# y of a gMLP encoder transposed by 32x32 blocks on all partitions at once, with transfers joining the quarters

## The chip, the core and the metric

The kernel runs on one core of one Trainium2 chip. The metric is the device time in microseconds of one execution; a kernel's time is the median of several. Profiles come from one further execution each. Engines are named as in the profile: PE (matrix multiply), PEld (its weight loads), DVE (vector engine), ACT (activations), POOL (which here issues transfers and little else), SP (which only issues transfers).

## What is computed

One layer of a gMLP encoder in float32: 1024 tokens, model width D = 2048, inner width E = 4096, eight groups of 512 channels, chunks of 128 tokens.

```python
h = rmsnorm(x, a_norm)
u, v, gate = split(h @ w_in, 3)          # w_in: (2048, 3 * 4096)
u = gelu(u)
v = rmsnorm(gelu(v), v_gain)
sv = einsum('gpq,bnqgc->bnpgc', w_s, v_chunks) + b_s    # per chunk n of 128 tokens, per group g
y = u * sv
x = x + (y * silu(gate)) @ w_out         # w_out: (4096, 2048)
out = rmsnorm(x, final_norm)
```

The output projection contracts over the 4096 channels. The matrix unit contracts over partitions, so y, which is made with tokens on partitions, is needed with channels on partitions.

## The kernel before, in words

Both large products are done as a Strassen product of 2x2 blocks: seven products `p` instead of eight, of sums and differences of blocks (`A_OF` and `B_OF` name the blocks; 11, 12, 21, 22). Every float32 operand is split into a high part that the matrix unit takes in its fast format (`hi`, made by ACT, L88) and a rest (`lo`, made by DVE, L89), and `mm3` (L93 to L95) multiplies hi x hi, hi x lo and lo x hi into the same bank. A **step** is one block of 256 rows of the contraction (two halves `u` of 128) for four chunks `m` of 128 tokens: 2 x 4 x 3 = 24 matmuls of 128x512.

The work runs in this order. Four strips make v; eight gate strips, one for each group g, make u and the gate of 512 channels each; each strip has 7 products of 4 steps. Then the output stage runs the seven products of `OUT_ORDER` for two column pairs s, 8 steps each. `advance(i)` prefetches the raw operands three steps ahead (`prefetch`) and splits those of two steps ahead (`feed`); SP issues the loads of weights, POOL those of y (`load_y`) and v. Instructions of an engine run in the order in which they were placed, so DVE's `w_lo` of a step stands behind whatever was placed before it.

In a gate strip the gate product of a half (512 tokens, four chunks m) is finished in the sixth or seventh product; then `apply_spatial` multiplies by w_s on PE and DVE forms y in place, one 128x512 instruction for each m (L325). After that y is transposed. A DVE transposition works on blocks of 32x32 within 32 partitions. `finish_y` does one 32-token part of one chunk with four instructions on 32 partitions each (L354), which put every block at its place in a full transpose: `yt` has channels on its 128 partitions and tokens in order along the row. When two chunks are done, one transfer of 512 KB on POOL's queue writes `yt` to `y_dram[g][half]` (L358), 128 partitions with runs of 256 tokens (1 KB).

The transpositions are not placed at once but put on the list `later` with a planned cost (L329: 16 items of 1.2 for a half, four instructions each). After each step `work(us)` takes items until the budget is used up: 2.3 in a gate strip and in the output stage for s = 1; for s = 0 it is 1.1 when the product's A operand is one block and 0.6 when it is a sum. In the output stage additions to the result (L492) are put ahead of them in the list. `load_y` (L143) asks, for the last group, whether all 32 writes of y have been issued, and if not places everything that is on the list.

Buffers of 4 KB a partition come in pools: "big" (25) for raw operands and output tiles, "ax" (16) for activations, operands of y and the transposed tiles, "hl" (6) for split weights, "sum" (3).

In the output stage `feed` splits y with the same `split` as the weights; `products` takes `ah[:, u, t]`, 128 consecutive tokens of chunk m, as the stationary operand.

Of the kernel before, what the change touches and what calls it, by code (L numbers as in the profile page):

```python
# [7 lines left out]
F32 = mybir.dt.float32  # L8
F32R = mybir.dt.float32r
AF = mybir.ActivationFunctionType  # L10
ALU = mybir.AluOpType
# [21 lines left out]
def gmlp_kernel(ctx, tc, x, xT, g_in, w_in, gain, wsT, bsT, w_out, fnorm, out):  # L33
# [9 lines left out]
    JI = D // P // 4  # L43
    JO = E // P // 4
    NV = G // 2
    AHEAD, LOADS = 2, 3

    main = ctx.enter_context(tc.tile_pool(name="main", bufs=1))
# [37 lines left out]
    def split(raw, hi, lo):  # L86

        nc.scalar.activation(out=hi, in_=raw, func=AF.Copy)  # L88
        nc.vector.tensor_tensor(out=lo, in0=raw, in1=hi.bitcast(F32), op=ALU.subtract)  # L89

    def mm3(acc, ah, al, bh, bl, start, stop, on=False):

        nc.tensor.matmul(out=acc, lhsT=ah, rhs=bh, start=start, stop=False, skip_group_check=on)  # L93
        nc.tensor.matmul(out=acc, lhsT=ah, rhs=bl, start=False, stop=False, skip_group_check=on)  # L94
        nc.tensor.matmul(out=acc, lhsT=al, rhs=bh, start=False, stop=stop, skip_group_check=on)  # L95
# [16 lines left out]
    steps += [("out", s, p, j) for p in OUT_ORDER for s in range(len(outs)) for j in range(JO)]  # L112

    v_dram = [[dram.tile([P, HCH, C], F32, tag=f"v{g}_{h}", name=f"v{g}_{h}") for h in range(2)] for g in range(G)]
    y_dram = [[dram.tile([P, CB, HT], F32, tag=f"y{g}_{h}", name=f"y{g}_{h}") for h in range(2)] for g in range(G)]
    a_dram = {(p, j): [dram.tile([P, 2, HT], F32, tag=f"a{p}_{j}{l}", name=f"a{p}_{j}{l}") for l in "hl"]
              for p in IN_ORDER for j in range(JI)}

# [3 lines left out]
    def load_w(step, block):  # L122
        kind, s, p, j = step
        mat, cols, n = (w_in, strips, JI) if kind == "in" else (w_out, outs, JO)
        cached = kind == "in" and (s > 0 or block == 22)
        key = (kind, s, 0 if cached else p, block, j)
        if key not in wraw:
            k = ((block // 10 - 1) * n + j) * 2 * P
            col = cols[s][block % 10 - 1]
            wraw[key] = slot("big", "w_raw")  # L130
            nc.sync.dma_start(
                out=wraw[key], in_=mat[k:k + 2 * P, col:col + C].rearrange("(u p) c -> p u c", p=P))
        return wraw[key]

    def load_y(step, block):
        _, _, p, j = step
        key = (p, block, j)
        if key not in yraw:
            g, b = divmod(((block % 10 - 1) * JO + j) * 2, CB)
            if g == G - 1 and pairs_of_y[0] < 4 * G:  # L140
                work_all()
            yraw[key] = slot("big", "y_raw")
            nc.gpsimd.dma_start(out=yraw[key], in_=y_dram[g][block // 10 - 1][:, b:b + 2, :])  # L143
        return yraw[key]

    def prefetch(i):
# [44 lines left out]
    def feed(i):  # L191

        if i >= len(steps):
            return
        kind, s, p, j = step = steps[i]
        first = kind == "in" and s == 0
        if first or (kind == "out" and s == 0):
            load = h_block if first else load_y
            raw = combine(A_OF[p], lambda b: load(step, b), "sum", "a_sum")


            out_j = j if kind == "out" else -1
            tag = "big" if (p == OUT_ORDER[0] and out_j >= JO - 4) or (p == OUT_ORDER[-1] and out_j == JO - 1) else "ax"
            parts = [slot(tag, f"a_{l}", F32R) for l in ("hi", "lo")]
            split(raw, *parts)
            aparts[i] = parts
            if first:
                for t, d in zip(parts, a_dram[p, j]):
                    nc.gpsimd.dma_start(out=d, in_=t.bitcast(F32))
        elif kind == "out":  # L210
            aparts[i] = aparts[i - JO]
        raw = combine(B_OF[p], lambda b: load_w(step, b), "sum", "w_sum")
        wparts[i] = [slot("hl", f"w_{l}", F32R) for l in ("hi", "lo")]
        split(raw, *wparts[i])
# [72 lines left out]
        inv_rms(ssv_t, E, rv)  # L287


    Q = 32  # L290
    spatial = {}

    def load_v(g, c):
# [22 lines left out]
    def apply_spatial(g, half, n_set, prod):  # L316
        banks = bank_set(n_set, f"sv{g}_{half}")
        for m in range(HCH):
            sv = banks[m // 2][:, m % 2]
            wh, wl, vh, vl = spatial[half * HCH + m]  # L320
            mm3(sv, wh, wl, vh, vl, True, True)
        for m in range(HCH):
            sv = banks[m // 2][:, m % 2]
            y = prod[m // 2][:, m % 2]
            nc.vector.scalar_tensor_tensor(  # L325
                out=y, in0=sv, scalar=bs_sb[:, g:g + 1], in1=y, op0=ALU.add, op1=ALU.mult)
        for m in range(HCH):
            for part in range(P // Q):
                later.append((1.2, lambda m=m, part=part: finish_y(g, half, m, part, prod[m // 2])))  # L329

    def spatial_step(k, g, cs, n_set):

# [10 lines left out]

    yts = {}

    def finish_y(g, half, m, i, y):

        t, c = divmod(m, 2)
        if c == 0 and i == 0:
            yts[0] = slot("ax", "y_t").rearrange("p a (b c) -> p (a b) c", c=2 * P)  # L350
        yt = yts[0]
        yv = y[:, c].rearrange("t (b q c) -> t b q c", b=CB, q=P // Q)
        for q in range(P // Q):
            nc.vector.transpose(  # L354
                out=yt[q * Q:(q + 1) * Q, :, c * P + i * Q:c * P + (i + 1) * Q],
                in_=yv[i * Q:(i + 1) * Q, :, q, :])
        if c == 1 and i == P // Q - 1:
            nc.gpsimd.dma_start(out=y_dram[g][half][:, :, 2 * t * P:2 * (t + 1) * P], in_=yt)  # L358
            pairs_of_y[0] += 1

    pairs_of_y = [0]


    def products(i, banks, fresh, ms=range(4)):
        _, _, p, j = steps[i]
        (ah, al), (bh, bl) = aparts[i], wparts[i]
        last = j == (JI if i < n_in else JO) - 1
        for u in range(2):
            for m in ms:
                t = slice(m * P, (m + 1) * P)  # L370
                mm3(banks[m // 2][:, m % 2], ah[:, u, t], al[:, u, t], bh[:, u], bl[:, u],
                    fresh and j == 0 and u == 0, last and u == 1, not fresh)

    def advance(i):
# [97 lines left out]


    NB = D // C
    sso = [main.tile([P, HCH, NB], F32, tag=f"sso{h}", name=f"sso{h}") for h in range(2)]
    acc = {}
    fn_b = []
# [2 lines left out]
    def init_acc(s, block):  # L480
        if (s, block) in acc:
            return
        acc[s, block] = [slot("big", f"o{block}_{t}") for t in range(2)]
        col = outs[s][block % 10 - 1]
        for t in range(2):
            r0 = ((block // 10 - 1) * HCH + 2 * t) * P
            nc.gpsimd.dma_start(
                out=acc[s, block][t], in_=x[r0:r0 + 2 * P, col:col + C].rearrange("(u p) c -> p u c", p=P))

    def add_to(s, block, sign, t, banks):  # L490
        d = acc[s, block][t]
# [26 lines left out]
    def finish_rows(h, m):  # L518

        ro = ros.pop((h, m))  # L520
        r0 = (h * HCH + m) * P
        for s in range(2):
            for n in range(2):
                block = 10 * (h + 1) + n + 1
# [5 lines left out]
                else:  # L530
                    nc.scalar.activation(out=d, in_=d, func=AF.Copy, scale=ro)
                col = outs[s][n]
                nc.sync.dma_start(out=out[r0:r0 + P, col:col + C], in_=d)

    n_set = a
    for p in OUT_ORDER:
# [91 lines left out]
```

## Time and profile before

| | |
|---|---|
| median of 3 runs | 2563.28 us (2563.18 to 2563.37) |
| profiled execution | 2561.8 us, its span 2560.0 us |
| mean granted clock of PE | 0.995 of full speed |
| busy: PE, PEld, DVE, ACT, POOL | 98%, 81%, 70%, 33%, 7% |
| moved by DMA | 695.62 MB, mean 272 GB/s |

The span runs from the first to the last instruction in the trace; the time of the execution is a little longer. Busy shares are averages over stages that differ. Matmuls are pipelined: each is recorded for longer than the distance to the next, so whether PE loses time is read from the distance between starts, not from its busy share. A wait is shown in brackets behind the row of the instruction that waited, with the engine and line that ended it.

### The profile page before, as it was taken

How to read it: one execution, taken by the hardware profiler on the slowest of the kernel's cores; microseconds unless marked ns; L12 is line 12 of the kernel's file. 1: busy time of each engine (PE TensorE's matmuls, PEld its weight loads, DVE VectorE, ACT ScalarE, POOL GpSimd, SP SyncE). 2: the span in 40 equal slices, each digit the busy share in tenths (PEclk: the TensorE clock that was granted, in tenths of full speed). 3: DMA queues.
4: the chain of work that ended last, by engine and by line, in shares of the span. 5: the costliest groups of instructions: out<-in, count | busy, mean ns of one | idle time of the engine just before them, and what ended most of it. 6: DMA issues, size and time to landing. Idle time of an engine off the chain costs nothing.

```text
span 2560.0 us, 29690 instructions
## 1 busy us (share of the span) xinstructions
PE 2514.0 (98%) x10980; PEld 2062.0 (81%) x10980; DVE 1797.8 (70%) x2469; ACT 856.3 (33%) x1008; POOL 167.3 (7%) x290
## 2 busy tenths in 40 slices
PE   7999999999999999999999999999999999999998
PEld 4878888888888888888888888888888788888886
DVE  7974544545448869588595886958769855576795
ACT  4542332323324242232423324233243232232342
POOL 1210000000000000000000000000010110010010
PEclk8999999999999999999999999999999999999999
DMA  8897785958767685766858668586696875678885
GB/s 316 315 411 286 274 313 201 381 204 329 281 254 272 230 336 200 288 260 241 328 203 294 253 242 336 194 307 248 223 362 209 298 257 173 223 263 284 298 294 189
DMA packets 246784, 695.62 MB, mean 272 GB/s; under 512 B 21472, under 2 KB 21488, under 8 KB 246640
## 3 DMA queue, kind: packets, MB, share of 16 engines
q1 hardware_dynamic: 207552, 551.62, 59.7%
q0 software_dynamic: 39088, 142.11, 15.0%
q8 instruction: 87, 1.43, 0.2%
q14 instruction: 57, 0.47, 0.1%
HBM read 622.34 MB, written 71.30 MB: 271 GB/s over the span
## 4 chain that ended last, share of the span: by engine, by line
PE 76%; DVE 16%; issue 5%; DMA 2%; ACT 1%; POOL 0%; SPq 0%; POOLq 0%; ACTq 0%; DVEq 0%
PE m L94 19%; PE m L93 18%; PE m L95 18%; DVE y_t L354 8%; PE o L94 7%; PE o L93 7%; PE o L95 7%; DVE w_lo L89 3%; DVE w_sum L103 1%; DMA w_raw<-in_w_in 1%; DVE c L325 1%; DMA y_raw<-y 1%; DVE u L431 0%; DVE c L411 0%; ACT w_hi L88 0%
## 5 line engine op out<-in xcount | busy, mean ns | idle before, releaser
L93 PE MATMUL m<-w_hi,a_hi 128*128 128x512 f32 x2688 | 1048.5, 390 | 9.4 <-DVE u L431 4.8
L94 PE MATMUL m<-w_lo,a_hi 128*128 128x512 f32 x2688 | 1049.4, 390 | 4.5 <-DVE w_lo L89 4.5
L95 PE MATMUL m<-w_hi,a_lo 128*128 128x512 f32 x2688 | 1047.9, 390 | 0.2 <-DVE a_lo L89 0.2
L89 DVE TENSOR_TENSOR w_lo<-w_sum,w_hi 128x1024 fp32r<-128x1024 f32 x320 | 391.1, 1222 | 402.9 <-ACT w_hi L88 402.0
L88 ACT ACTIVATE w_hi<-w_sum 128x1024 fp32r<-128x1024 f32 x320 | 339.0, 1060 | 954.2 <-PE m L94 668.9
L93 PEld LDWEIGHTS m<-w_hi,a_hi 128*128 128x128 f32 x2688 | 505.8, 188 | 117.8 <-issue 6.6
L94 PEld LDWEIGHTS m<-w_lo,a_hi 128*128 128x128 f32 x2688 | 505.8, 188 | 114.8 <-DVE w_lo L89 9.8
L95 PEld LDWEIGHTS m<-w_hi,a_lo 128*128 128x128 f32 x2688 | 505.6, 188 | 105.8 <-DVE a_lo L89 0.9
L103 DVE TENSOR_TENSOR w_sum<-w_raw 128x1024 f32<-128x1024 f32 x320 | 389.7, 1222 | 100.5 <-DMA w_raw<-in_w_in 88.3
L94 PE MATMUL o<-w_lo,a_hi 128*128 128x512 f32 x896 | 349.6, 390 | 6.0 <-DVE w_lo L89 6.0
L93 PE MATMUL o<-w_hi,a_hi 128*128 128x512 f32 x896 | 348.7, 389 | 0.8 <-DVE o L575 0.8
L95 PE MATMUL o<-w_hi,a_lo 128*128 128x512 f32 x896 | 348.7, 389 | 0.0
L354 DVE STREAM_TRANSPOSE y_t<-c 32x128 f32<-32x128 f32 x1024 | 309.9, 303 | 15.1
L88 ACT ACTIVATE w_hi<-w_raw 128x1024 fp32r<-128x1024 f32 x128 | 135.9, 1061 | 451.2 <-PE m L94 348.7
L89 DVE TENSOR_TENSOR w_lo<-w_raw,w_hi 128x1024 fp32r<-128x1024 f32 x128 | 155.6, 1216 | 132.8 <-ACT w_hi L88 131.9
L94 PEld LDWEIGHTS o<-w_lo,a_hi 128*128 128x128 f32 x896 | 168.2, 188 | 44.0 <-DVE w_lo L89 9.3
L93 PEld LDWEIGHTS o<-w_hi,a_hi 128*128 128x128 f32 x896 | 168.2, 188 | 36.4 <-DVE o L575 1.5
L95 PEld LDWEIGHTS o<-w_hi,a_lo 128*128 128x128 f32 x896 | 168.2, 188 | 34.7
L88 ACT ACTIVATE a_hi<-a_sum 128x1024 fp32r<-128x1024 f32 (+1 forms) x61 | 63.7, 1044 | 146.4 <-DVE a_sum L103 137.0
L143 POOL DMA_DIRECT2D y_raw<-y x96 | 50.9, 531 | 467.0 <-DVE w_sum L103 245.6
L89 DVE TENSOR_TENSOR a_lo<-a_sum,a_hi 128x1024 fp32r<-128x1024 f32 (+1 forms) x61 | 73.3, 1202 | 10.1 <-ACT a_hi L88 10.1
L358 POOL DMA_DIRECT2D y<-y_t x32 | 23.1, 721 | 727.5 <-DVE y_t L354 727.5
(91 smaller groups left out, 1108.2 us busy)
## 6 DMA issues: line engine op xcount, KB each, us to landing
w_raw<-in_w_in SPq DMA_DIRECT2D x212, 512.0 KB, 6.7
w_raw<-in_w_out SPq DMA_DIRECT2D x192, 512.0 KB, 6.4
y_raw<-y POOLq DMA_DIRECT2D x96, 512.0 KB, 6.3
a_hi<-a_0h SPq DMA_DIRECT2D x77, 512.0 KB, 4.9
a_lo<-a_0l SPq DMA_DIRECT2D x77, 512.0 KB, 5.5
a_hi<-a_1h SPq DMA_DIRECT2D x77, 512.0 KB, 6.4
a_lo<-a_1l SPq DMA_DIRECT2D x77, 512.0 KB, 5.1
a_hi<-a_2h SPq DMA_DIRECT2D x77, 512.0 KB, 6.0
```

Of the source, the lines that this page charges most:

```text
L88: nc.scalar.activation(out=hi, in_=raw, func=AF.Copy)
L89: nc.vector.tensor_tensor(out=lo, in0=raw, in1=hi.bitcast(F32), op=ALU.subtract)
L93: nc.tensor.matmul(out=acc, lhsT=ah, rhs=bh, start=start, stop=False, skip_group_check=on)
L94: nc.tensor.matmul(out=acc, lhsT=ah, rhs=bl, start=False, stop=False, skip_group_check=on)
L95: nc.tensor.matmul(out=acc, lhsT=al, rhs=bh, start=False, stop=stop, skip_group_check=on)
L103: nc.vector.tensor_tensor(out=s, in0=a, in1=b, op=ALU.add if of[1] > 0 else ALU.subtract)
L143: nc.gpsimd.dma_start(out=yraw[key], in_=y_dram[g][block // 10 - 1][:, b:b + 2, :])
L325: nc.vector.scalar_tensor_tensor(out=y, in0=sv, scalar=bs_sb[:, g:g + 1], in1=y, op0=ALU.add, op1=ALU.mult)
L354: nc.vector.transpose(out=yt[q * Q:(q + 1) * Q, :, c * P + i * Q:c * P + (i + 1) * Q], in_=yv[i * Q:(i + 1) * Q, :, q, :])
L358: nc.gpsimd.dma_start(out=y_dram[g][half][:, :, 2 * t * P:2 * (t + 1) * P], in_=yt)
```

## The change

`finish_y` now takes a whole chunk m (128 tokens on 128 partitions) and transposes it with two DVE instructions of 128 partitions x 256 channels each, one for each half n of the group's channels. Each 32x32 block is transposed within its 32 partitions, so partition 32 q + c holds channel c of a block, and tokens 32 q to 32 q + 31 of the chunk. Two tiles (n = 0, 1) collect the four chunks of a half. At the end eight transfers, one for each n and each quarter q of 32 partitions, write 128 KB each in runs of 128 tokens (512 B) to `y_dram`, where the channels of the quarters come together in one row: a row of channel c holds its 512 tokens in the order (q, m, t), t being the token within 32.

`y_dram[g][half]` becomes a plain array of 512 channels x 512 tokens. A load of y puts rows 2p and 2p+1 of a block of 256 on partition p, and so the rows of w_out are loaded in the same order; weights of the first product are loaded as before. `split_y` splits y and puts tokens in order at the same time: ACT writes `hi` in the order (m, u, q, t) with runs of 32, DVE reads the raw tile in runs of 32. `products` takes its 128 tokens of chunk m from that order. In `later` a half has 4 items with a planned cost of 0.8 instead of 16 of 1.2. The accesses to x and out are written with other views of the same rows.

```diff
+    def split_y(raw, hi, lo):
+        rv_, hv = [t.rearrange("p u (q m t) -> p (u q) m t", m=HCH, t=Q) if t is raw else
+                   t.rearrange("p a b -> p (a b)").rearrange("p (m n t) -> p n m t", m=HCH, t=Q) for t in (raw, hi)]
+        nc.scalar.activation(out=hv, in_=rv_, func=AF.Copy)
+        rm, hm, lm = rv_.rearrange("p n m t -> p m n t"), hv.rearrange("p n m t -> p m n t"), None
+        lm = lo.rearrange("p a b -> p (a b)").rearrange("p (m n t) -> p m n t", m=HCH, t=Q)
+        nc.vector.tensor_tensor(out=lm, in0=rm, in1=hm.bitcast(F32), op=ALU.subtract)
...
-    y_dram = [[dram.tile([P, CB, HT], F32, tag=f"y{g}_{h}", name=f"y{g}_{h}") for h in range(2)] for g in range(G)]
+    y_dram = [[dram.tile([C, HT], F32, tag=f"y{g}_{h}", name=f"y{g}_{h}") for h in range(2)] for g in range(G)]
...
-                out=wraw[key], in_=mat[k:k + 2 * P, col:col + C].rearrange("(u p) c -> p u c", p=P))
+            order = "(u p) c -> p u c" if kind == "in" else "(p u) c -> p u c"
+            nc.sync.dma_start(out=wraw[key], in_=mat[k:k + 2 * P, col:col + C].rearrange(order, p=P))
...
-            if g == G - 1 and pairs_of_y[0] < 4 * G:
+            if g == G - 1 and halves_of_y[0] < 2 * G:
                 work_all()
...
-            nc.gpsimd.dma_start(out=yraw[key], in_=y_dram[g][block // 10 - 1][:, b:b + 2, :])
+            nc.gpsimd.dma_start(
+                out=yraw[key], in_=y_dram[g][block // 10 - 1][b * P:(b + 2) * P].rearrange("(p u) t -> p u t", p=P))
...
-            split(raw, *parts)
+            (split if first else split_y)(raw, *parts)
...
         for m in range(HCH):
-            for part in range(P // Q):
-                later.append((1.2, lambda m=m, part=part: finish_y(g, half, m, part, prod[m // 2])))
+            later.append((0.8, lambda m=m: finish_y(g, half, m, prod[m // 2][:, m % 2])))
...
+    def finish_y(g, half, m, y):
+        if m == 0:
+            yts[0] = [slot("ax", f"y_t{n}").rearrange("p a (b c) -> p (a b) c", c=P) for n in range(2)]
+        yv = y.rearrange("t (n b c) -> t n b c", n=2, c=Q)
+        for n in range(2):
+            nc.vector.transpose(out=yts[0][n][:, :, m * Q:(m + 1) * Q], in_=yv[:, n])
+        if m == HCH - 1:
+            yd = y_dram[g][half].rearrange("(n b c) t -> n c b t", n=2, c=Q)
+            for n in range(2):
+                for q in range(P // Q):
+                    nc.gpsimd.dma_start(out=yd[n, :, :, q * P:(q + 1) * P], in_=yts[0][n][q * Q:(q + 1) * Q])
+            halves_of_y[0] += 1
...
+        at = [t.rearrange("p a (m c) -> p a m c", c=P) if i < n_in else
+              t.rearrange("p a b -> p (a b)").rearrange("p (m a c) -> p a m c", a=2, c=P) for t in (ah, al)]
...
-                mm3(banks[m // 2][:, m % 2], ah[:, u, t], al[:, u, t], bh[:, u], bl[:, u],
+                mm3(banks[m // 2][:, m % 2], at[0][:, u, m], at[1][:, u, m], bh[:, u], bl[:, u],
```

## Rows read from the trace of the kernel before

**Rows 1.** The page, part 1: busy us (share of the span) x instructions.
```profile
PE 2514.0 (98%) x10980; PEld 2062.0 (81%) x10980; DVE 1797.8 (70%) x2469; ACT 856.3 (33%) x1008; POOL 167.3 (7%) x290
```

**Rows 2.** Timeline of PE, 1000 to 1012 us: start, duration, instruction, [wait].
```profile
1000.09 0.39 PE L93 MATMUL m<-w_hi,a_hi 128*128 128x512 f32 x1
...
1004.40 0.39 PE L94 MATMUL m<-w_lo,a_hi 128*128 128x512 f32 x1
...
1011.65 0.39 PE L93 MATMUL m<-w_hi,a_hi 128*128 128x512 f32 x1
```

**Rows 3.** Busy time by stretch: length, PE, PEld, DVE, ACT, POOL, clock, DMA share.
```profile
820.00:2050.00 1230.00, 1219.50 (x5355) 1003.11 (x5354) 964.72 (x1633) 394.62 (x415) 59.96 (x97) 1.00 0.73 266
2050.00:2540.00 490.00, 490.00 (x2163) 405.88 (x2162) 330.17 (x309) 156.67 (x193) 46.09 (x81) 1.00 0.72 249
```

**Rows 4.** PE's waits, whole span: us in total, times, longest.
```profile
PE o L94 <- DVE w_lo L89: 6.0, 6, 2.0
...
PE m L94 <- DVE w_lo L89: 4.5, 7, 0.7
```

**Rows 5.** Timeline of PE, a gate strip's late operand.
```profile
1025.93 0.39 PE L93 MATMUL m<-w_hi,a_hi 128*128 128x512 f32 x1
...
1032.63 0.50 PE L94 MATMUL m<-w_lo,a_hi 128*128 128x512 f32 x1 [0.66 <-DVE w_lo L89]
...
1037.98 0.39 PE L93 MATMUL m<-w_hi,a_hi 128*128 128x512 f32 x1
```

**Rows 6.** Timeline of DVE, the same strip.
```profile
996.65 3.79 DVE L354 STREAM_TRANSPOSE y_t<-c 32x128 f32<-32x128 f32 x12
1000.47 1.22 DVE L89 TENSOR_TENSOR w_lo<-w_raw,w_hi 128x1024 fp32r<-128x1024 f32 x1
...
1026.21 2.84 DVE L354 STREAM_TRANSPOSE y_t<-c 32x128 f32<-32x128 f32 x9
1029.09 1.22 DVE L431 TENSOR_TENSOR u<-u,m 128x1024 f32<-128x1024 f32 x1
...
1031.36 1.22 DVE L89 TENSOR_TENSOR w_lo<-w_raw,w_hi 128x1024 fp32r<-128x1024 f32 x1
```

**Rows 7.** Timeline of PE, the output stage's first products.
```profile
1979.53 0.39 PE L93 MATMUL o<-w_hi,a_hi 128*128 128x512 f32 x1
...
2018.24 0.50 PE L94 MATMUL o<-w_lo,a_hi 128*128 128x512 f32 x1 [2.03 <-DVE w_lo L89]
...
2058.63 0.39 PE L93 MATMUL o<-w_hi,a_hi 128*128 128x512 f32 x1
```

**Rows 8.** Timeline of DVE, the output stage before its longest wait.
```profile
1994.49 3.79 DVE L354 STREAM_TRANSPOSE y_t<-c 32x128 f32<-32x128 f32 x12
...
2014.69 1.23 DVE L103 TENSOR_TENSOR a_sum<-y_raw 128x1024 f32<-128x1024 f32 x1 [4.40 <-DMA y_raw<-y]
...
2016.97 1.22 DVE L89 TENSOR_TENSOR w_lo<-w_sum,w_hi 128x1024 fp32r<-128x1024 f32 x1
```

**Rows 9.** Timeline of POOL, the same place.
```profile
2001.09 1.06 POOL L143 DMA_DIRECT2D y_raw<-y  x2 [1.79 <-DVE w_sum L103]
```

**Rows 10.** Groups of instructions: out<-in, shapes, count | busy us, mean ns | idle before.
```profile
L354 DVE STREAM_TRANSPOSE y_t<-c 32x128 f32<-32x128 f32 x1024 | 309.9, 303 | 15.1
...
L325 DVE SCALAR_TENSOR_TENSOR c<-sv,bs_sb,c 128x512 f32<-128x512 f32 x64 | 43.6, 742 | 0.0
...
L311 DVE SCALAR_TENSOR_TENSOR ws_hl<-ws_sb,rv,ws_hl 128x128 fp32r<-128x128 f32 x64 | 19.4, 344 | 0.0
...
L143 POOL DMA_DIRECT2D y_raw<-y x96 | 50.9, 531 | 467.0 <-DVE w_sum L103 245.6 <-PE m L95 70.6 <-DVE a_sum L103 61.7
...
L358 POOL DMA_DIRECT2D y<-y_t x32 | 23.1, 721 | 727.5 <-DVE y_t L354 727.5
```

**Rows 11.** DMA: a queue's packets, MB, share; issues with KB each, us to landing.
```profile
q0 software_dynamic: 39088, 142.11, 15.0%
...
y<-y_t POOLq DMA_DIRECT2D x32, 512.0 KB, 4.6
```

More of the change, by code (lines that the diff above doesn't have):

```diff
@@ L45, in gmlp_kernel @@
     NV = G // 2
+    Q = 32
     AHEAD, LOADS = 2, 3
@@ L130, in load_w @@
             wraw[key] = slot("big", "w_raw")
-            nc.sync.dma_start(
-                out=wraw[key], in_=mat[k:k + 2 * P, col:col + C].rearrange("(u p) c -> p u c", p=P))
+            order = "(u p) c -> p u c" if kind == "in" else "(p u) c -> p u c"
+            nc.sync.dma_start(out=wraw[key], in_=mat[k:k + 2 * P, col:col + C].rearrange(order, p=P))
         return wraw[key]
@@ L287, in finish_rv @@
         inv_rms(ssv_t, E, rv)
-    Q = 32
     spatial = {}
@@ L344, in gmlp_kernel @@
     yts = {}
[L346 to L361, printed above, removed]
+    def finish_y(g, half, m, y):
[10 more added lines that the diff above has]
+            halves_of_y[0] += 1
+    halves_of_y = [0]
     def products(i, banks, fresh, ms=range(4)):
@@ L367, in products @@
         last = j == (JI if i < n_in else JO) - 1
+        at = [t.rearrange("p a (m c) -> p a m c", c=P) if i < n_in else
+              t.rearrange("p a b -> p (a b)").rearrange("p (m a c) -> p a m c", a=2, c=P) for t in (ah, al)]
         for u in range(2):
             for m in ms:
-                t = slice(m * P, (m + 1) * P)
-                mm3(banks[m // 2][:, m % 2], ah[:, u, t], al[:, u, t], bh[:, u], bl[:, u],
+                mm3(banks[m // 2][:, m % 2], at[0][:, u, m], at[1][:, u, m], bh[:, u], bl[:, u],
                     fresh and j == 0 and u == 0, last and u == 1, not fresh)
@@ L474, in gmlp_kernel @@
     NB = D // C
+    xv, ov = [r.rearrange("(h t u p) d -> h t p u d", h=2, t=2, p=P) for r in (x, out)]
     sso = [main.tile([P, HCH, NB], F32, tag=f"sso{h}", name=f"sso{h}") for h in range(2)]
@@ L485, in init_acc @@
         for t in range(2):
-            r0 = ((block // 10 - 1) * HCH + 2 * t) * P
-            nc.gpsimd.dma_start(
-                out=acc[s, block][t], in_=x[r0:r0 + 2 * P, col:col + C].rearrange("(u p) c -> p u c", p=P))
+            nc.gpsimd.dma_start(out=acc[s, block][t], in_=xv[block // 10 - 1, t, :, :, col:col + C])
     def add_to(s, block, sign, t, banks):
@@ L520, in finish_rows @@
         ro = ros.pop((h, m))
-        r0 = (h * HCH + m) * P
         for s in range(2):
@@ L532, in finish_rows @@
                 col = outs[s][n]
-                nc.sync.dma_start(out=out[r0:r0 + P, col:col + C], in_=d)
+                nc.sync.dma_start(out=ov[h, m // 2, :, m % 2, col:col + C], in_=d)
     n_set = a
```

## The prediction

> **What bounds the kernel now.** I read the page's busy shares first, then TensorE's own timeline, then who made it wait, then VectorE's timeline around those places. PE is busy for 98% of the span and DVE for 70% [rows 1], but a busy PE says little, since matmuls overlap in the records; what counts is the distance between their starts. In an undisturbed stretch 51 starts follow each other in 1011.65 - 1000.09 = 11.56 us, that is 0.2267 us each [rows 2]. A step of 24 matmuls is then 5.44 us. Once y is transposed, from 2050 to 2540 us, PE is busy for 490.00 of 490.00 us; in the part where y is transposed, 820 to 2050 us, it is busy for 1219.50 of 1230.00 [rows 3]. The 10.5 us that are missing there have one releaser: DVE's w_lo, 4.5 us in seven waits of the gate strips and 6.0 us in six waits of the output stage [rows 4]. What else PE loses lies at the head and the tail, which the change doesn't touch.
>
> The waits alone understate the loss, because the pipeline also has to fill again. In a gate strip, from the step that starts at 1025.93 to the one at 1037.98 are 48 matmuls, or 10.88 us at the pitch; it took 12.05, so 1.17 us are lost around one wait of 0.66 [rows 5]. Seven strips repeat this: 7 x 1.17 = 8.2 us. In the output stage, 1979.53 to 2058.63 are 13 steps, 13 x 5.44 = 70.7 us at the pitch, and took 79.1: 8.4 us lost [rows 7]. Together **16.6 us** is the most that this change can give back.
>
> Why w_lo is late is seen on DVE. Before the late w_lo of 1031.36 it ran 9 transpositions until 1029.05, then the update of u (1029.09), a w_sum, and only then w_lo [rows 6]; none of these waited for anything, they stood in line. The planner books 1.2 us for four transpositions and takes two such items a step, so 32 items of a strip (128 transpositions) take more steps than there are between the two halves, and the queue lasts until the next update of u.
>
> **What the change removes, adds and moves.**
> DVE: 1024 transpositions of 128 elements on 32 partitions go, 309.9 us, 303 ns each [rows 10]. 128 transpositions of 256 elements on 128 partitions come. No row has one. Low end: two forms of one operation, 128 and 512 elements wide, take 344 and 742 ns [rows 10], 1.04 ns an element; 303 + 128 x 1.04 = 436 ns. High end, if time simply followed elements: 606 ns. An operation on 128 partitions with 128 elements takes 344 ns, close to the 303 ns on 32 partitions, so I read the time as following elements and not partitions, and take 0.44 us: 128 x 0.44 = 56 us (78 at the high end). DVE loses some 250 us of work, 19 us a half down to 3.5.
> The Trainium skill, page "VectorE: DVE Perf Modes", section "The three transpose paths", gives 311 ns for a VectorE transposition of 128x128 (bf16); as an estimate from that page, 256 elements would come to 311 + 133 = 0.44 us and the sum would be the same. No run here shows it yet.
>
> Planner: a half gives 4 items of 0.8 instead of 16 of 1.2. With a budget of 2.3 a step takes three items, 6 x 0.44 = 2.6 us, where it took 8 x 0.316 = 2.5 us; the first step of a burst is as full as before, and the second has one item instead of two. The burst is over after two steps instead of some eight. So the queue ahead of u is gone when it matters: 2.84 us of transpositions stood directly before the late operand, against a wait of 0.66 [rows 5, 6]. **Strips: all 8.2 us.**
>
> Output stage: DVE's transpositions of the last group's two halves reach far into it; with two items a step from a budget of 1.1 they end two steps after the second half is applied, before the queue that still stands at 1994 now [rows 8]. Five of the six waits stand behind transpositions and the additions to the output; without the first, the second fit (w_sum and w_lo 2.4 us, one or two additions of 1.2, inside 5.44). They go. The sixth, 2.03 us, is different: w_lo of 2016.97 stood behind an a_sum that waited 4.40 us for its y_raw [rows 7, 8]. That load was issued late, in a chain whose first link, at 2001.09, waited 1.79 us for a w_sum that 12 transpositions (3.79 us) had held up [rows 8, 9]. Part of it is therefore the transpositions' doing, part the number of buffers, which does not change. With its refill it costs 2.03 + 0.5 = 2.6 us; I leave 1.3 of them. **Output stage: 8.4 - 1.3 = 7.1 us.**
>
> POOL: 32 issues of 721 ns (512 runs each) go, 128 come, of 256 runs. Loads of 128 runs take 531 ns [rows 10], so 0.53 to 0.73 each; 68 to 93 us instead of 23, on an engine busy for 7% [rows 1]. Eight in a row hold POOL's queue for 4 to 6 us, once a half. Behind them stand the loads of v for the next group, used more than 60 us later, and in the output stage the loads of y and x; the last eight are issued two steps after the second half is applied, ahead of the second product's loads of y. I cost this at nothing; without that cover it is up to 6 us, once.
>
> Transfers: the same 16.8 MB, in runs of 512 B instead of 1 KB and from 32 partitions at a time. The software queue took 15.0% of 2560 us for 142.11 MB, 2.7 us a MB [rows 11], so y takes some 45 us of all engines' time now. If a transfer from a quarter of the partitions ran at a quarter of the rate, it would be 181 us, 136 more in 1230 us: the busy share goes from 0.73 to 0.84 [rows 3]. No matmul waits for a transfer in this stretch, so nothing; below nothing is possible too, since what DVE frees earlier is loaded earlier.
>
> Splitting y: ACT and DVE read or write in runs of 32 instead of 512, in 56 splits. The nearest row is the transposition itself, which reads such runs and takes 303 ns for 128 elements, less than the 344 ns of an operation that reads one run [rows 10]. I take nothing; the upper end is a doubling, 1.2 us a split. w_out is loaded with rows 2p and 2p+1 on partition p, in runs of the same length, and x and out are only written differently in the code: nothing for each.
>
> Two buffers for the transposed half are held at once, and not one, but for two steps and a landing (4.6 us [rows 11]) instead of eight steps; product buffers come free earlier. Each load of y now waits for eight transfers of its half; only the last group's are young, and they are written earlier than now.
>
> **Sum.** 8.2 + 7.1 = 15.3 us. The profiled execution took 2561.8 us (span 2560.0), 1.5 us under the median of 2563.28; I carry the difference over: 2563.28 - 15.3 = **2548.0 us**.
>
> **Rivals.**
> Only the strips gain (0.12). The output stage's waits are a matter of buffers: DVE still waits for y_raw and w_lo stands behind it [rows 8]. For it: the 4.40 us. Against: five of six waits had no transfer ahead. 2563.3 - 8.2 = 2555.1 us.
> No gain (0.09). Splitting in runs of 32 doubles a_lo. In the three last passes both operands are sums and DVE has 4.9 us of four operations a step; 6.1 exceeds 5.44 by 0.7 in 24 steps, 16 us, which eats the gain: 2563 us. Against it: the 303 ns of the transposition.
> Slower, by the transposition (0.04). If the four groups of 32 partitions are worked one after another, an instruction takes 4 x 606 ns = 2.42 us. The first step of a burst then has 6 x 2.42 = 14.5 us. Its w_lo (1000.47, done at 1001.69) is wanted at 1004.40 [rows 2, 6]: 2.7 us of slack, and 3.79 us of transpositions already stand before it. A stall is 14.5 - 3.8 - 2.7 = 8.0 us, in 16 halves 128 us: 2563 + 128 - 15 = 2676 us. It decides from 1.24 us an instruction on, where 16 x (6 x 1.24 - 6.5) equals the gain.
> Slower, by the transfers (0.05). If each of the 128 transfers holds all engines for the whole 4.6 us that a y transfer now takes to land [rows 11], they need 589 us instead of 45; 0.73 x 1230 + 544 = 1442 us do not fit into 1230, 212 us more: about 2760 us. It decides from 0.27 x 1230 = 332 us extra, that is 2.9 us of exclusive time a transfer. Against it: the 2.7 us a MB above, 0.35 us for 128 KB.
> The Trainium skill, page "DMA: Bandwidth & Descriptors", section "Rules for kernel authors", speaks against this change in just this place: it advises one transfer over 128 partitions instead of several over parts of them, and to join small transfers into a large one. By that rule this rival would be nearer than I rank it; the trace of before has no such transfer and decides neither way.
>
> **How the numbers follow.** Forecast 0.70 (2546.7, with all 16.6 us, to 2552), strips alone 0.12, no gain 0.09, slower 0.09 in two parts. About 0.2%, 5.1 us, is what a measurement of this kernel can tell from no change. Faster by more: 0.70 + 0.12 = 0.82; within: 0.09; slower: 0.09. The range runs from 2546.4 (all of it, and 0.3 of spread) to 2555.5, which takes in the strips' case.
>
> **What would show it.** Right: transpositions near 0.44 us, 128 of them; no wait of PE for w_lo between 860 and 1980; a step pitch of 5.44 us through 1025 to 1038; at most one wait left in the output stage, behind a y_raw. Wrong: a transposition above 1.1 us, a_lo above 1.3 us, a DMA share near 1, or the same waits with other work standing before w_lo.

## The result, and the profile after

The kernel after takes 2548.13 us (median of four runs, 2547.66 to 2548.61); the kernel before, beside it, 2563.32 us (2563.18 to 2564.04). The ratio is 0.994 with a 95% interval of 0.9923 to 0.9957: faster, by 15.2 us. The prediction was 2548.0 us.

Page of the kernel after: busy us (share of the span) x instructions, a DMA queue (packets, MB, share of 16 engines), and the chain that ended last by engine.

```profile
PE 2507.7 (98%) x10980; PEld 2064.5 (81%) x10980; DVE 1535.1 (60%) x1573; ACT 855.3 (34%) x1008; POOL 218.4 (9%) x386
...
q0 software_dynamic: 40624, 142.12, 15.1%
...
PE 96%; DVE 2%; DMA 1%; issue 0%; ACT 0%; POOL 0%; SPq 0%; POOLq 0%; ACTq 0%; DVEq 0%
```

DVE lost 262.7 us of work [rows 1], POOL gained 51, and the software queue takes the share that it took [rows 11]. PE is as busy as before, 98%, which is why that line says nothing of the gain. The stretch in which y is transposed does.

Busy time by stretch, kernel after (columns as in [rows 3]).

```profile
820.00:2050.00 1230.00, 1230.00 (x5429) 1018.80 (x5428) 708.88 (x753) 397.83 (x419) 107.94 (x188) 1.00 0.75 269
```

PE is busy for all of 1230.00 us, where it was for 1219.50 [rows 3]. Its waits, whole span (us in total, times, longest):

```profile
PE ss_x L262 <- DVE sq_x L261: 9.0, 7, 6.7
PE ss_x L277 <- DVE d_x L275: 7.1, 2, 6.4
PE m L103 <- DVE u L444: 6.1, 1, 6.1
PE m L103 <- ACT a_hi L89: 4.1, 1, 4.1
PE o L103 <- DVE o L586: 0.8, 1, 0.8
PE m L103 <- DVE u L437: 0.5, 1, 0.5
```

No line names w_lo any more; both of [rows 4] are gone. What is left are the head and one wait in the last product. The timeline of PE, kernel after: the same two steps of the gate strip as in [rows 5], and the same 13 steps of the output stage as in [rows 7].

```profile
1027.02 0.39 PE L103 MATMUL m<-w_hi,a_hi 128*128 128x512 f32 x1
...
1037.90 0.39 PE L103 MATMUL m<-w_hi,a_hi 128*128 128x512 f32 x1
...
1973.58 0.39 PE L103 MATMUL o<-w_hi,a_hi 128*128 128x512 f32 x1
...
2044.30 0.39 PE L103 MATMUL o<-w_hi,a_hi 128*128 128x512 f32 x1
```

The 48 matmuls take 1037.90 - 1027.02 = 10.88 us, the pitch; before it was 12.05. The 13 steps take 70.72 us, where it was 79.1. The timeline of DVE, kernel after, shows why: one burst of a half and the update of u that follows, then the place in the output stage that answers to [rows 8].

```profile
988.48 2.72 DVE L336 SCALAR_TENSOR_TENSOR c<-sv,bs_sb,c 128x512 f32<-128x512 f32 x4
991.11 2.72 DVE L364 STREAM_TRANSPOSE y_t<-c 128x256 f32<-128x256 f32 x8
995.45 1.23 DVE L90 TENSOR_TENSOR w_lo<-w_raw,w_hi 128x1024 fp32r<-128x1024 f32 x1 [1.61 <-ACT w_hi L89]
...
1020.42 1.22 DVE L444 TENSOR_TENSOR u<-u,m 128x1024 f32<-128x1024 f32 x1 [1.99 <-PE m L105]
...
1997.90 1.23 DVE L113 TENSOR_TENSOR a_sum<-y_raw 128x1024 f32<-128x1024 f32 x1 [2.75 <-DMA y_raw<-y]
...
2000.18 1.22 DVE L90 TENSOR_TENSOR w_lo<-w_sum,w_hi 128x1024 fp32r<-128x1024 f32 x1
```

The eight transpositions of a half are over in 2.72 us, in one row. The update of u, which stood in line behind nine transpositions [rows 6], now waits 1.99 us for PE: DVE is ahead of PE there, not behind it.

**Where PE's time goes.** For every two matmuls that follow each other I took the distance of their starts less 0.2267 us, and added this up by stretch (distances in which a matmul record is missing left out). The table has all the profiles of this study; "four times" and "eight times" are kernels of the next section. The gate strips stand up to 1930 us, the first products of the output stage from 1930 to 2100 us; with eight times, and in the kernel before placed at once, the strips last longer.

| profile | head, to 150 us | strips | output stage | last matmul to the end |
|---|---|---|---|---|
| before | 36.55 | 8.21 | 8.37 | 10.75 |
| before, again | 36.91 | 8.18 | 8.51 | 10.74 |
| after | 38.41 | 0 | 0 | 11.78 |
| after, again | 37.98 | 0 | 0 | 11.84 |
| after, 1024 transpositions | 36.06 | 6.93 | 13.78 | 11.78 |
| after, two times | 37.87 | 0 | 0 | 11.81 |
| after, four times | 36.60 | 0 | 8.55 | 11.81 |
| after, four times, again | 38.38 | 0 | 8.62 | 11.82 |
| after, eight times | 36.88 | 104 | 28 | 11.77 |
| after, transfers three times | 37.47 | 0 | 0 | 10.89 |
| after, spread | 37.99 | 0 | 0 | 11.81 |
| after, u first in the head | 37.69 | 0 | 0 | 11.82 |
| before, placed at once | 36.08 | 136 | 28 | 10.72 |

The 8.2 and the 8.4 us of the prediction's first part are all given back. The head differs by up to 2.3 us and the tail by 1.1, in places that the change does not touch by design; the experiments come back to both. In the kernels with new waits, part of the loss is not in the waits themselves: behind some of them the matmuls start 0.43 us apart for a while instead of 0.23.

### The profile page after: what moved, and what is told of

It is laid out like the page before. It is cut to its first block, busy times and chain, and to the rows that moved or that the text cites. A ratio compares the mean times of both kernels' runs of the same rounds, so it can differ in the third digit from the quotient of the medians.

```text
span 2546.7 us, 28921 instructions
## 1 busy us (share of the span) xinstructions
PE 2507.7 (98%) x10980; PEld 2064.5 (81%) x10980; DVE 1535.1 (60%) x1573; ACT 855.3 (34%) x1008; POOL 218.4 (9%) x386
## 3 DMA queue, kind: packets, MB, share of 16 engines
q0 software_dynamic: 40624, 142.12, 15.1%
## 4 chain that ended last, share of the span: by engine, by line
PE 96%; DVE 2%; DMA 1%; issue 0%; ACT 0%; POOL 0%; SPq 0%; POOLq 0%; ACTq 0%; DVEq 0%
PE m L103 24%; PE m L104 24%; PE m L105 24%; PE o L103 8%; PE o L104 8%; PE o L105 8%; DMA w_raw<-in_w_in 1%; PE sv L104 1%; PE sv L103 1%; PE sv L105 1%; DVE x_t L183 0%; DVE w_lo L90 0%; DVE a_lo L90 0%; DVE sq_x L261 0%; SPq L257 0%
## 5 line engine op out<-in xcount | busy, mean ns | idle before, releaser
L103 PE MATMUL m<-w_hi,a_hi 128*128 128x512 f32 x2688 | 1048.7, 390 | 10.7 <-DVE u L444 6.1
L369 POOL DMA_DIRECT2D y<-y_t x128 | 74.0, 586 | 400.8 <-DVE y_t L364 397.2
L96 ACT ACTIVATE a_hi<-a_sum 128x1024 fp32r<-128x1024 f32 x40 | 42.3, 1058 | 100.5 <-DVE a_sum L113 100.5
L444 DVE TENSOR_TENSOR u<-u,m 128x1024 f32<-128x1024 f32 x46 | 56.0, 1219 | 31.4 <-PE m L105 29.9
L307 POOL DMA_DIRECT2D v_raw<-v x32 | 17.4, 544 | 660.5 <-DVE ws_hl L322 644.5
```

Source lines behind the costliest of these rows:

```text
L96: nc.scalar.activation(out=hv, in_=rv_, func=AF.Copy)
L307: nc.gpsimd.dma_start(out=spatial["v", c], in_=v_dram[g][h][:, 2 * t:2 * t + 2])
L369: nc.gpsimd.dma_start(out=yd[n, :, :, q * P:(q + 1) * P], in_=yts[0][n][q * Q:(q + 1) * Q])
L444: soon.append((1.2, lambda t=t: nc.vector.tensor_tensor(out=cs["u"][t], in0=cs["u"][t], in1=banks[t], op=ALU.subtract)))
```

## The experiments

The theory (A): PE waited for a w_lo that stood in DVE's queue behind transpositions, and the change gains because their work in that queue falls from 310 to 44 us. The rivals: the new layout and its transfers gain by themselves (B); the place of the items in the planner's list does it, since the list is empty early, whatever the work (C); and what the prediction had feared, that transfers or a longer transposition cost something that is only hidden.

**1024 transpositions again, in the new layout.** The kernel after, with four transpositions of 32x128 in each of 16 items of a half.

```diff
-            later.append((0.8, lambda m=m: finish_y(g, half, m, prod[m // 2][:, m % 2])))
+            for part in range(P // Q):
+                later.append((1.2, lambda m=m, part=part: finish_y(g, half, m, prod[m // 2][:, m % 2], part)))
...
-        for n in range(2):
-            nc.vector.transpose(out=yts[0][n][:, :, m * Q:(m + 1) * Q], in_=yv[:, n])
+        n, bs = part // 2, slice(part % 2 * 4, part % 2 * 4 + 4)
+        for q in range(P // Q):
+            ps_ = slice(q * Q, (q + 1) * Q)
+            nc.vector.transpose(out=yts[0][n][ps_, bs, m * Q:(m + 1) * Q], in_=yv[ps_, n, bs])
```

> The changed kernel with the kernel before's DVE work put back: each chunk is transposed by 16 instructions of 32 partitions x 128 elements (1024 in all) instead of 2 of 128 x 256, in 16 list items of 1.2 a half as before; layout, transfers, splitting and the loads of w_out stay changed. Theory A (PE was late because some 20 us of transpositions a half stood in DVE's queue ahead of w_lo): the 13 waits for w_lo return, 2563 us (2560 to 2567), DVE busy near 1800 us. Theory B (the gain comes from the changed layout, transfers or splitting): 2548 us, no wait for w_lo.

Measured: 2565.97 us (2563.62 to 2569.34) against 2562.07 for the kernel before, ratio 1.0013 (1.0004 to 1.0023). The gain is gone. PE's waits and then DVE's timeline at a strip, of this kernel:

```profile
PE m L104 <- DVE w_lo L90: 4.6, 7, 0.7
PE o L104 <- DVE w_lo L90: 4.5, 4, 1.8
...
PE o L105 <- DVE a_lo L99: 2.4, 1, 2.4
PE o L103 <- ACT w_hi L89: 1.9, 1, 1.9
```

```profile
1025.27 2.91 DVE L367 STREAM_TRANSPOSE y_t<-c 32x128 f32<-32x128 f32 x9
1028.21 1.22 DVE L447 TENSOR_TENSOR u<-u,m 128x1024 f32<-128x1024 f32 x1
1029.35 1.22 DVE L113 TENSOR_TENSOR w_sum<-w_raw 128x1024 f32<-128x1024 f32 x1
1030.48 1.22 DVE L90 TENSOR_TENSOR w_lo<-w_raw,w_hi 128x1024 fp32r<-128x1024 f32 x1
```

The seven waits of the strips are back with their size, behind the same nine transpositions, update of u and w_sum as in [rows 6], though layout, transfers and splits are those of the kernel after. So the strips speak for A, and not for B. In the output stage this kernel loses 5.4 us more than the kernel before (13.78 against 8.37). New is a wait of 2.4 us for an a_lo, and 13 matmuls, here and behind the wait for w_hi, that start 0.43 us apart (the granted clock from 1945.3 to 1953 us is 0.81 in the mean), which cost 2.6 us more; the kernel before has none such in its output stage. What part of the order or the buffers makes the wait was not tried and stays open. The new layout alone brings nothing.

**Each transposition several times.** The kernel after, with the DVE instruction repeated 2, 4 or 8 times.

```diff
         for n in range(2):
-            nc.vector.transpose(out=yts[0][n][:, :, m * Q:(m + 1) * Q], in_=yv[:, n])
+            for _ in range(4):
+                nc.vector.transpose(out=yts[0][n][:, :, m * Q:(m + 1) * Q], in_=yv[:, n])
```

> The changed kernel with every transposition done four times over into the same place, in the same list items of 0.8. Eight now run in 2.72 us, so a half costs DVE 10.9 us instead of 2.7, still half of the kernel before's 20 us. Theory A with the slack read in the changed trace (w_lo after the first half's burst is ready some 4.5 us before its step, after the second half's some 9): the first halves stall 8.2 - 4.5 = 3.7 us and a refill of 0.5, 8 of them, about 33 us: 2580 us (2560 to 2600). By the prediction's formula, 6d - 6.5 with d = 1.36 us, 16 halves: 2548 + 26 + 8 = 2582 us. If only the total of DVE's work counts (theory D): DVE stays below 70% and the time at 2548 us.

Measured: 2555.01 us (2554.34 to 2555.88), ratio 0.9972 (0.9962 to 0.9983): 7 us more than the kernel after, about a fifth of what was expected. Its waits for operands in the stretch of y, and its timelines of DVE and PE at a burst:

```profile
PE o L103 <- ACT w_hi L89: 2.5, 2, 2.1
PE o L104 <- DVE w_lo L90: 2.1, 2, 1.5
```

```profile
989.13 7.94 DVE L365 STREAM_TRANSPOSE y_t<-c 128x256 f32<-128x256 f32 x24
996.99 1.18 DVE L90 TENSOR_TENSOR w_lo<-w_raw,w_hi 128x1024 fp32r<-128x1024 f32 x1
```

```profile
1003.27 0.39 PE L103 MATMUL m<-w_hi,a_hi 128*128 128x512 f32 x1
1003.50 0.39 PE L104 MATMUL m<-w_lo,a_hi 128*128 128x512 f32 x1
```

The strips lose nothing. After 7.94 us of transpositions the w_lo is done at 998.17 and wanted at 1003.50, with 5.3 us to spare. What is lost, 8.6 us in both profiles of this kernel, lies in the first products of the output stage, where the last group's transpositions meet w_sum, a_lo and w_lo; 2.6 us of it are again 13 matmuls that start 0.43 us apart.

> The changed kernel with every transposition done twice. A half costs DVE 5.4 us, a burst of eight becomes 2.7 us longer, less than the 4.5 us by which the next w_lo is early. Theory A with slack: no wait, 2548 us (2546 to 2550). If every us on DVE in these stretches costs PE time in proportion to the kernel before (16.6 us for 266 us of work), 44 us more would cost 2.7 us: 2551 us.

With two times: 2547.56 us (2545.43 to 2548.15), ratio 0.9942 (0.9927 to 0.9956), no wait for w_lo. DVE's extra 42 us cost nothing, as A with slack says; a loss in proportion is not there.

> The kernel after with each transposition issued eight times, some 2.65 us for one place (8 x 0.33 us). It tests how much DVE work a half can take before PE waits. By the rival's formula in the prediction (stall = 6 d - 6.5 us a half, 16 halves) this is 9.4 us a half, 150 us: about 2697 us. With the slack read from the kernel with four times (from the start of a burst at 989.13 to the start of the matmul that wants the late w_lo at 1003.50, less 1.2 us for w_lo itself, is 13.2 us, against 6 d = 15.9), 2.7 us a half in the first step of a burst, some 1 us more in the second (two transpositions, 5.3 us, and a w_lo in a step of 5.44), and 0.5 for the refill: 4 us x 14 halves = 60 us, and 20 to 30 us in the output stage's beginning: 2610 to 2640 us. If the work in DVE's queue were not what PE waits for, 2548 us.

With eight times: 2678.65 us in one run, beside 2562.6. It lies between the two numbers expected, nearer to the formula's. Waits, then timelines of PE and of DVE in one strip, and the busy time around its long wait:

```profile
PE m L104 <- DVE w_lo L90: 78.3, 17, 9.2
```

```profile
997.07 0.63 PE L104 MATMUL m<-w_lo,a_hi 128*128 128x512 f32 x1 [2.14 <-DVE w_lo L90]
...
1031.95 0.80 PE L104 MATMUL m<-w_lo,a_hi 128*128 128x512 f32 x1 [8.48 <-DVE w_lo L90]
```

```profile
980.12 15.79 DVE L365 STREAM_TRANSPOSE y_t<-c 128x256 f32<-128x256 f32 x48
...
1007.82 2.35 DVE L425 TENSOR_TENSOR c<-c,u 128x1024 f32<-128x1024 f32 x2
...
1015.00 15.78 DVE L365 STREAM_TRANSPOSE y_t<-c 128x256 f32<-128x256 f32 x48
1030.71 1.18 DVE L90 TENSOR_TENSOR w_lo<-w_raw,w_hi 128x1024 fp32r<-128x1024 f32 x1
```

```profile
1023.00:1048.00 25.00, 16.52 (x68) 13.20 (x67) 21.11 (x47) 3.01 (x3) 6.24 (x11) 0.86 0.49 160
```

A strip has two bursts, and they differ. The first has the slack that was read from the kernel with four times, 13.2 us: 2.7 us of wait were expected, 2.14 came. At the second DVE is still late from the first, since between them it has no idle time to catch up; from the burst's start at 1015.00 to 1023.47, when PE began to wait, are 8.5 us, less 1.2 for w_lo 7.3 us. That is near the 6.5 of the prediction's formula, and 15.8 us overrun it by 8.5. And 104 us are lost in the strips around 78.3 us of waits. Some 18 us of the difference are 91 matmuls that start about 0.43 us apart, behind such waits; in the stretch shown the granted clock is 0.86 in the mean while PE works for 16.52 of 25 us. Neither of the two numbers expected had a term for this. The rest, some 7 us, lies around the same waits.

**Transfers three times.** The kernel after, with each of the 128 transfers of y issued to two more tensors in DRAM.

```diff
                     nc.gpsimd.dma_start(out=yd[n, :, :, q * P:(q + 1) * P], in_=yts[0][n][q * Q:(q + 1) * Q])
+                    for z in spare:
+                        zd = z[g][half].rearrange("(n b c) t -> n c b t", n=2, c=Q)
+                        nc.gpsimd.dma_start(out=zd[n, :, :, q * P:(q + 1) * P], in_=yts[0][n][q * Q:(q + 1) * Q])
```

> The changed kernel with two more copies of y written to spare places in DRAM by the same 128 KB transfers, 384 instead of 128. The rows price y at 45 us of all DMA engines, so 90 us more in 1230 us: the DMA share of that stretch goes from 0.75 to 0.82, POOL issues 14 us in a row per half instead of 4.6. Transfers cost nothing (the prediction): 2548 us (2546 to 2551). If each transfer held all engines as long as it takes to land (5.6 us): 256 x 5.6 = 1434 us more, over 3600 us. A value between shows what the 128 transfers cost.

Measured: 2546.72 us (2545.98 to 2547.23), ratio 0.9939 (0.9925 to 0.9954). Busy time and queue of this kernel:

```profile
820.00:2050.00 1230.00, 1230.00 (x5429) 1018.80 (x5428) 707.91 (x753) 397.24 (x418) 252.45 (x439) 1.00 0.83 296
```

```profile
q0 software_dynamic: 52912, 175.69, 18.8%
```

256 more transfers raise the DMA share of the stretch from 0.75 to 0.83 and POOL's busy time from 108 to 252 us, and PE loses nothing. The queue takes 18.8% of 2544.7 instead of 15.1% of 2546.7 us, 94 us more for 33.57 MB: 2.8 us a MB, 0.37 us of all engines for a transfer of 128 KB. The rival with 4.6 us each was off by a factor of twelve.

**Spread.** The kernel after, with eight items of a planned cost of 2.4, one transposition each, so that the planner takes one a step.

```diff
-            later.append((0.8, lambda m=m: finish_y(g, half, m, prod[m // 2][:, m % 2])))
+            for n in range(2):
+                later.append((2.4, lambda m=m, n=n: finish_y(g, half, m, prod[m // 2][:, m % 2], n)))
```

> The changed kernel with its 8 transpositions of a half spread one to a step (8 list items of 2.4, each over the step's budget), so that the list empties as late as in the kernel before, with 0.34 us a step instead of 2.5. Theory A (work in the queue): 2548 us (2546 to 2550). Theory C (what helped is that the list is empty before the next products' additions and updates): the waits come back, towards 2563 us. The last half's transfers are issued later, so the output stage could lose up to 5 us in either.

Measured: 2547.96 us (2546.61 to 2548.2), ratio 0.9943 (0.9929 to 0.9958); PE is busy for 1230.00 of 1230.00 us. But the transpositions did not run one a step. DVE's timeline of this kernel, the second half of a strip:

```profile
995.87 0.44 DVE L364 STREAM_TRANSPOSE y_t<-c 128x256 f32<-128x256 f32 x1
...
1001.31 2.40 DVE L364 STREAM_TRANSPOSE y_t<-c 128x256 f32<-128x256 f32 x7
```

They are over after 8 us; those of a first half run as 2, 4 and 2 within 6.3 us. So what was to be tested, a late end of the list with little work in it, came about only in part and in the last group alone, and this run decides nothing between A and C. It also shows that the order on DVE is not the list's step by step: in the strip of [rows 6], in both profiles of the kernel before, 12, 1, 15, 1, 22, 6, 10 and 9 transpositions stand between its other instructions, where the list gives out eight a step. The planned costs shape that order, but do not set it; what else does was not tried.

**Before, placed at once.** The kernel before, with items of a planned cost of 0.15, so that a half's 64 transpositions fall into one step.

```diff
-                later.append((1.2, lambda m=m, part=part: finish_y(g, half, m, part, prod[m // 2])))
+                later.append((0.15, lambda m=m, part=part: finish_y(g, half, m, part, prod[m // 2])))
```

> The kernel before with its list items costed at 0.15 instead of 1.2, so that all 64 transpositions of a half are placed at once: the same 1024 instructions, the list as short as in the changed kernel. Theory A (work in the queue): a burst of 20 us against a slack of 4.5 to 9 us stalls PE some 11 to 15 us in each of 16 halves: 2700 to 2800 us. Theory C (the early empty list is what helped): near 2548 us.

Measured: 2711.64 us (2709.86 to 2713.41), ratio 1.0584 (1.0562 to 1.0605). Waits, busy time and a burst of this kernel:

```profile
PE m L94 <- DVE w_lo L89: 96.8, 14, 7.3
PE o L94 <- DVE w_lo L89: 11.3, 3, 9.5
```

```profile
820.00:2050.00 1230.00, 1133.20 (x4826) 930.62 (x4825) 845.33 (x1419) 354.95 (x377) 41.03 (x66) 0.95 0.67 239
```

```profile
1016.98 20.23 DVE L354 STREAM_TRANSPOSE y_t<-c 32x128 f32<-32x128 f32 x64
```

The same 310 us of transpositions, only earlier, cost some 150 us more; 36 us of PE's loss lie in 179 matmuls that start about 0.43 us apart. Here the list did end early, with all 64 transpositions in one row, and the loss grew. So C falls: not the early end of the list, but the work that stands before w_lo. Whether another placing, with fewer transpositions a step or all of them behind w_lo, would have gained something with the old operation was not tried.

**The head.** The kernel after, with the operands of a later step prepared behind the first update of u and not ahead of it, in the last step of each product of the first strip.

```diff
+                behind = s == 0 and j == JI - 1
+                if behind:
+                    prefetch(i + LOADS)
+                else:
+                    advance(i)
...
+            if s == 0:
+                work(0)
+                feed(i - 1 + AHEAD)
```

> The changed kernel with one edit in the first strip alone: in the last step of each product the operands of the step after next are split only after the product's result has been taken from its banks, so that DVE's update of u (L444) does not stand behind a w_sum that waits for a weight transfer. In the changed trace PE waits 6.1 us for that update and then runs 12 matmuls at half the pitch, 2.3 us. If the order on DVE is the cause: 2540 to 2544 us. If the head is bound by the transfers: the wait appears at the next w_lo instead, 2546 to 2550 us.

Measured: 2548.68 us (2547.83 to 2549.77), ratio 0.9949 (0.9932 to 0.9966), no gain. PE's wait in the head, this kernel:

```profile
PE m L103 <- DVE u L444: 6.7, 1, 6.7
```

The wait is as long as it was, at the same place. DVE ahead of it:

```profile
134.23 1.23 DVE L113 TENSOR_TENSOR w_sum<-w_raw 128x1024 f32<-128x1024 f32 x1 [3.73 <-DMA w_raw<-in_w_in]
...
136.50 2.35 DVE L444 TENSOR_TENSOR u<-u,m 128x1024 f32<-128x1024 f32 x2
```

A w_sum that waits 3.73 us for its weights still stands ahead of the update. So the edit did not bring about the order that it was meant to try, and neither of the two things expected is shown.

**The head's spread.** Two kernels once more, unchanged, for a second profile: the kernel before, and four times the transpositions.

> The kernel before, once more, for its profile: PE's loss in the head (before 150 us). If the head's 1.9 us that the kernel after lost more (38.4 against 36.6 us above the pitch) are a matter of the execution, this profile can lie anywhere between 36 and 38.5; if they belong to the kernel, it lies at 36.0 to 36.8, with a wait for the first update of u of 4.5 to 4.8 us.

> The kernel with four times the transpositions, once more, for its profile: the head and the output stage. Its head lost 36.6 us, though its instructions there are those of the kernel after (38.4 and 38.0 us in two profiles). If the head varies by execution, this one can lie anywhere between 36 and 38.5; if it belongs to the kernel, at 36.6 again. The strips lose nothing and the output stage 6 to 7 us, as before.

They took 2562.32 and 2557.09 us. The kernel before lost 36.91 us in its head, just above what was expected if the loss belonged to the kernel, with a wait of 5.6 us for the first update of u, longer than the 4.8 of its other profile. The kernel with four times is clearer: 36.60 us in one profile and 38.38 in the other (its output stage lost 8.62 us, where 6 to 7 were expected). The same kernel covers 1.8 of the 2.3 us, so the 1.9 us between the profiles of before and after in the table need not be the change's; whether the new code loses more in the mean is not settled. The tail: three profiles of the old code have 10.7 us from the last matmul to the end, nine of the new code 11.8, and one of the new code 10.9. But the last transfer lands 8.6 us after the last matmul in old and new code alike (9.2 in the kernel with eight times, whose tail is 11.8 like the others'). The 1.1 us lie behind that landing, where the traces show no work of the program any more; what sets them stays open.

A second set of runs of the kernel after gave 2547.7 us (2546.37 to 2547.89), ratio 0.9943 (0.9928 to 0.9957).

## Why the prediction was right

**What bounded the kernel.** Right, and shown: DVE's late w_lo was PE's only loss between 800 and 2060 us, 16.6 us of it, and it went when the transpositions went, came back with them though layout and transfers stayed new, and stayed away with three times the transfers.

**The transposition.** Estimated at 0.44 us. The groups of the kernel after (out<-in, shapes, count | busy us, mean ns | idle before), and the counterpart of one of them in the kernel before:

```profile
L369 POOL DMA_DIRECT2D y<-y_t x128 | 74.0, 586 | 400.8 <-DVE y_t L364 397.2 <-issue 1.9 <-DVE w_lo L90 1.8
...
L364 DVE STREAM_TRANSPOSE y_t<-c 128x256 f32<-128x256 f32 x128 | 43.6, 406 | 0.0
...
L99 DVE TENSOR_TENSOR a_lo<-y_raw,a_hi 128x1024 fp32r<-128x1024 f32 x16 | 19.4, 1217 | 0.0
```

```profile
L89 DVE TENSOR_TENSOR a_lo<-y_raw,a_hi 128x1024 fp32r<-128x1024 f32 x16 | 19.4, 1219 | 0.4 <-ACT a_hi L88 0.3
```

The 406 ns are a mean: the first of a row has 0.43 us, those behind it 0.40, and one that stands alone in the spread kernel 0.44. So the low end, 303 + 128 x 1.04 = 436 ns, is what a single one takes; in a row of eight it is 2.72 us, 0.34 each, and the 128 took 43.6 us instead of 56. Four times the partitions and twice the elements together cost no more than the prediction gave to the elements; no run changes one of the two alone. The Trainium skill, page "VectorE: DVE Perf Modes", section "The three transpose paths", from which the prediction worked out the same estimate of 0.44 us, fits: the trace has 0.44 us for one that stands alone.

**The planner.** Six transpositions in a step and two in the next were counted on; in the strips all eight ran in one row (991.11). With 2.72 us for the eight nothing came of it, but the count for a step was not a reading of DVE's order, and in the kernel before it was not one either: that instructions run in the order in which they were placed holds there only roughly.

**Strips: 8.2 us.** Right, as 7 x 1.17: the table's 8.21 is now 0.

**Output stage: 7.1 us.** The term was mis-sized: all 8.4 us came. The 1.3 us that were left for an a_sum waiting for its y_raw are not needed. The a_sum at 1997.90 still waits, 2.75 us instead of 4.40 [rows 8], and the w_lo behind it, at 2000.18, comes some 3.7 us later than the rhythm of the steps before it would have it; but it is done at 2001.40, and the matmul that wants it starts at 2006.44: 5.0 us are left. The wait for the transfer was harmful only on top of a queue that was already late.

**POOL.** 586 ns each, 74.0 us, inside the range of 68 to 93, and costed at nothing rightly: eight issues in a row hold the queue for 4.60 us, and no matmul waits for what stands behind them.

**Transfers.** The estimate of a DMA share up to 0.84 was a bound; it went to 0.75. The trace shows no price for the rule that spoke against the change: the Trainium skill, page "DMA: Bandwidth & Descriptors", section "Rules for kernel authors", advises against splitting a transfer by partitions and against small ones. Each transfer now lands 5.6 us after its issue, though it carries a quarter of what took 4.6 [rows 11]; but the queue's share of the engines is 15.1% after 15.0%, and with three times as many transfers the kernel is no slower. Here the reader comes much later than the writer.

**Splitting, w_out, buffers.** Costed at nothing, rightly: a_lo of a y_raw takes 1217 ns where it took 1219. With that the rival "no gain" (a doubled a_lo) is out; "only the strips" is out by the output stage's 0.

**The rival of a long transposition.** Its condition did not come (406 ns, not 2.42 us), but its formula could be tried. At four times, 1.32 us for one place, it asks for 1.4 us of stall in each half; the strips had none, though at that length the rival left nothing of the gain and 7 us of it were left. At eight times it gives 2697 us; 2678.65 were measured. The slack of 6.5 us a burst was read at the w_lo of 1000.47 [rows 6]. DVE's timeline of the kernel before, just ahead of it:

```profile
985.76 6.97 DVE L354 STREAM_TRANSPOSE y_t<-c 32x128 f32<-32x128 f32 x22
992.76 1.23 DVE L89 TENSOR_TENSOR w_lo<-w_raw,w_hi 128x1024 fp32r<-128x1024 f32 x1
```

The w_lo before it had itself stood behind 22 transpositions of the strip's first half; the queue was late already. The 6.5 us hold for such places only, as for the second burst of a strip at eight times; a burst that starts on time has 13.2 us. So the break-even of 1.24 us an instruction was too low, and the rival less likely than it looked.

**The sum.** 15.3 us were predicted and 15.2 measured, which is closer than the terms are, and in part luck. PE's loss in the strips and the output stage fell by 16.6 us, 1.3 more than the sum. The two profiles differ by 2560.0 - 2546.7 = 13.3 us: in the kernel after the first matmul starts 0.4 us later, the head loses 1.9 more and the tail 1.1, places to which the prediction gave nothing. And beside the kernel before in the later runs (2561.84 us) the second set of the kernel after gained 14.1 us.

## What to carry to other kernels

When PE waits for an operand that did not itself wait for anything, count what stands before it in its engine's queue; shortening that work pays up to the sum of the lost pitch, and other waits in a queue that is no longer late may then cost nothing, as that for y_raw here. Read the order from the engine's timeline, not from the planner's list. Here one instruction over all partitions replaced eight over a quarter of them, with half the elements each, at little more than the price of one; that is worth a trial even if the layout must be repaired later: where transfers and a split that runs anyway can reorder the data, the repair may cost nothing. And read slack at a place where the queue is on time, since slack read behind a late queue is too small for any other place.

## What the runs showed of the hardware

A float32 transposition by 32x32 blocks took 303 ns on 32x128 elements, and on 128x256 elements 436 ns where it stood alone; in a row, 9 of the first took 2.84 us [rows 6] and 8 of the second 2.72: eight times the elements for 8% more time each (0.316 and 0.340 us). Repeats that write the same place follow each other as closely (48 in 15.79 us, 0.33 us each).

A transfer from 32 partitions in runs of 512 B took 2.8 us of all DMA engines for a MB, against 2.7 for the queue's mean [rows 11]. Its issue on POOL took 586 ns for 256 runs, between 531 for 128 and 721 for 512 [rows 10]. The queue counts 48 packets for such a transfer ((52912 - 40624) / 256), not one for each run.

In the kernel with eight times, PE had stood still for 8.48 us until 1031.95; from there to 1034.67 its matmuls start 0.43 us apart instead of 0.23, which is the lower of the clock's two levels (1.2 and 2.4 GHz), and from 1034.98 on 0.23 again. The granted clock is 0.82 in the mean from 1032 to 1040 us and 1.00 from 1040 to 1048.
